# The high and low part of a weight side by side, and new start addresses for the moving operands

## The chip, the cores and the metric

The kernel runs on one core of one Trainium2 chip. The metric is the device time of one execution, in microseconds (us); three runs of the kernel before took 1782.89 to 1786.75 us, with a median of 1783.85 us.

## What is computed

The input is 512 tokens of 1024 channels, in float32. They pass a first block of two layers (a gated short convolution or latent attention with 8 heads, and each time a feed-forward part of width 2816 with a convolution over tokens) and a second block (three mixers side by side, then the same kind of feed-forward part). Nearly all of the work is in products of a weight matrix with the 512 tokens:

```python
def short_conv_mixer(x_n, w_in, conv_w, w_out):
    b, c, h = jnp.split(x_n @ w_in, 3, axis=-1)
    return (b * causal_dwconv(c * h, conv_w)) @ w_out

def conv_ffn(x_n, w_up, conv_w, w_down):
    g, u = jnp.split(causal_dwconv(x_n @ w_up, conv_w), 2, axis=-1)
    return (jax.nn.silu(g) * u) @ w_down
```

The largest are the three feed-forward parts, each with `w_up` of 1024 x 5632 and `w_down` of 2816 x 1024; then `a_w_in` (1024 x 3072), `a_w_out`, the projections of the attention (`w_dq`, `w_dkv`, `w_uq`, `w_ukv`, `w_o`) and of the second block (`w_in`, `w_out`).

## The kernel before

Channels lie on the 128 partitions and the 512 tokens along the free dimension, so an activation of 1024 channels is 8 tiles of 128 x 512. TensorE multiplies float32r operands, a rounded form of float32. To keep the precision, every operand is split into a high part (rounded to float32r) and a low part (the rest, also float32r), and a product is made of three matmuls in `mm3` (lines 157 to 159): high weight by high activation, low weight by high activation, high weight by low activation. In most products the weight is the stationary operand (128 x 128) and the activation the moving one (128 x 512); in `gemm_tok`, in `gating_in` and for the values in `layer_b` the roles are exchanged and the weight is moving.

Weights come through `slab`. A DMA on SyncE's queue brings up to 2048 columns into one of two `raw` buffers; the slab is then taken in pieces. For each piece ScalarE (ACT) casts `raw` into `whi` (line 147), and VectorE (DVE) subtracts `whi` from `raw` and writes `wlo` (line 149). `whi` and `wlo` are two tiles of the pool `wsp`, which has two buffers of each, and every word follows the one before it at a distance of 4 bytes. A piece of `w_up` has 1024 columns and feeds 24 matmuls, one of `w_down` has 1408 and feeds 33. Some pieces go to pools of their own instead (the argument `pool`): those are weights that must stay longer, such as the last pieces of a feed-forward part.

Activations that move through TensorE lie in the pool `xs` (the input of an up-projection, tiles `xsh` and `xsl`) and in `hid` (the input of a down-projection, `hidh` and `hidl`). The helper `pad` allocates a few bytes in front of a pool so that the next one begins at an address of choice; in the kernel before every moving operand and every weight tile begins at a multiple of 256 bytes. ACT and DVE also do the rest of the feed-forward part: the scaling, the convolution (line 282), the gate, the splits (lines 126 and 131), and in the first two feed-forward parts a matrix-vector product with `w_ada` on DVE (line 469).

The order of the instructions of each engine is made by a scheduler from priorities and a simulated timeline, not written by hand.

Of the kernel before, what the change touches and what calls it, by code (L numbers as in the profile page):

```python
# [12 lines left out]
F32R = mybir.dt.float32r  # L13
# [5 lines left out]
P = 128  # L19
# [10 lines left out]
PIECE = 1408  # L30
# [17 lines left out]
class Builder:  # L48
# [83 lines left out]
        else:  # L132
            self.done = nc.vector.scalar_tensor_tensor(vl, src, scale, vf, ALU.mult, ALU.subtract).ins

    def slab(self, src, piece, pool=None, width=PIECE):
        nc = self.nc
        n = src.shape[-1]
        raw = self.wraw.tile([P, SLAB], F32, tag="raw", name="raw")
        nc.sync.dma_start(raw[:, :n], src)
        for o in range(0, n, piece):  # L140
            own = pool[o // piece] if type(pool) is tuple else pool or self.wsp
            hi = own.tile([P, width], F32R, tag="whi", name="whi")
            lo = own.tile([P, width], F32R, tag="wlo", name="wlo")
            m = min(piece, n - o)
            s = slice(o, o + m)
            with self.tc.issue_after(self.rounded) if self.hold else nullcontext():
                nc.scalar.copy(hi[:, :m], raw[:, s])  # L147
            with self.tc.issue_after(self.hold) if self.hold else nullcontext():
                nc.vector.tensor_tensor(lo[:, :m], raw[:, s], hi[:, :m].bitcast(F32), ALU.subtract)  # L149
            if pool is None:  # L150
                yield hi, lo
            else:
                yield hi, lo, m
# [378 lines left out]
    def layer_b(self):  # L532
        nc = self.nc
        with ExitStack() as ctx:
# [27 lines left out]
            with ExitStack() as c2:  # L562
                v_pool = self.pool("v", 8, c2)
                k_pool, q_pool, r_pool = self.pool("k", 8, c2), self.pool("q", 8, c2), self.pool("r", 4, c2)
                self.ph = self.pool("ph_b2", 2, c2)
                o_pool = self.pool("o", 8, c2)

                def project(pr):
                    ks, vs, qs = [], [], []
                    for i, (wh, wl) in enumerate(self.slab(self.dr["w_uq"][pr], 512)):  # L570
                        ps = self.ps()
                        for k in range(4):
                            o = k * P
                            self.mm3(ps, wh[:, o:o + P], wl[:, o:o + P], *cq[k], k == 0, k == 3)
                        if i == 0:
                            x = self.t("sq", 2, self.tmp)
                            nc.scalar.copy(x, ps)
                        else:
                            qs.append(self.split(ps, q_pool, "q"))
                    (wh, wl), = self.slab(self.dr["w_ukv"][pr], 1024)  # L580
                    for i in range(2):
                        ps = self.ps()
                        for k in range(2):
                            o = (2 * i + k) * P
                            self.mm3(ps, wh[:, o:o + P], wl[:, o:o + P], *ckv[k], k == 0, k == 1)
                        ks.append(self.split(ps, k_pool, "k"))
                    for b in range(4):
                        ps = self.ps()[:, :256]
                        for k in range(2):
                            o = 512 + 256 * k  # L590
                            ch, cl = (t[:, b * P:(b + 1) * P] for t in ckv[k])
                            self.mm3(ps, ch, cl, wh[:, o:o + 256], wl[:, o:o + 256], k == 0, k == 1)
                        v = v_pool.tile([P, T], F32R, tag="v", name="v")
                        self.split_to(ps, v[:, :256], v[:, 256:])
                        vs.append(v)
                    qr = self.split(self.rope(x, cos, sin, self.done), r_pool, "r")
                    return ks, vs, qs, qr

                ready, outs = project(0), None
                for pr in range(5):  # L600
                    start = self.tc.tile_snap_priority()
                    mine = ready
                    if pr < 3:
                        ready = project(pr + 1)
                    if outs:
                        self.gemm(self.dr["w_o"], outs, self.add_h, (pr - 1,), 4)
                    if pr == 4:
                        break
                    ks, vs, qs, qr = mine
                    outs = []  # L610
                    with self.before(start):
                        for i in range(2):
                            r = slice(64 * i, 64 * i + 64)
                            outs.append(self.attend(qs[i], (qr[0][r], qr[1][r]), ks[i], (krh[r], krl[r]),
                                                    [(v[:, i * P:(i + 1) * P], v[:, 256 + i * P:256 + (i + 1) * P])
                                                     for v in vs], mask, o_pool))
# [54 lines left out]
    def gemm_tok(self, w, xs, n, kp, tok):  # L671

        ps = [self.ps() for _ in range(4)]
        k = 0
        for s in range(w.shape[0]):
            for hi, lo in self.slab(w[s], kp * n):
                for j in range(kp):
                    o = slice(j * n, j * n + n)
                    for b in range(4):
                        self.mm3(ps[b][:, :n], tok(xs[k][0], b), tok(xs[k][1], b), hi[:, o], lo[:, o],  # L680
                                 k == 0, k == KC - 1)
                    k += 1
        return ps
# [432 lines left out]
    def last_phase(self, y_b, wq, held, first, wf0, ctx):  # L1116

        with ctx:
            self.stat = self.pool("stat2", 1, ctx, space=PSUM)
            self.psum = self.pool("psum_f2", 7, ctx, space=PSUM)  # L1120
            self.xs = self.pool("xs2", 16, ctx)
            wf = self.pool("w_f", 1, ctx)
            add = self.summed(self.add_gated(16))
            n = 3 * P
            w = self.dr["w_out_b"]
# [46 lines left out]
    def ffn_phase(self, i, ctx):  # L1172
        self.stat = self.pool(f"stat{i}", 1, ctx, space=PSUM)
        with ExitStack() as ctx:
            self.xs = self.pool(f"xs{i}", 16, ctx)
            self.psum = self.pool(f"psum_f{i}", 7, ctx, space=PSUM)
            self.hid = self.pool(f"hid{i}", 28 - i, ctx)
            self.pad(480, ctx, side="right")
            self.ph = self.pool(f"ph_f{i}", 1, ctx, side="right")
# [129 lines left out]
```

## Time and profile before

| | |
|---|---|
| median of three runs | 1783.85 us |
| the execution that was profiled | 1781.47 us |
| its span from first to last instruction | 1779.5 us |
| TensorE matmul (PE) busy | 1749.2 us, 98% of the span |
| weight loads (PEld) busy | 1443.9 us, 81% |
| VectorE (DVE) busy | 1110.6 us, 62% |
| ScalarE (ACT) busy | 698.3 us, 39% |
| mean granted TensorE clock | 0.994 of full speed |

The profiled execution took 1.97 us more than its span. Matmuls overlap, and the length that the profile gives to one is modelled; what a matmul really costs in a stream is the distance from its start to the start of the next one. That distance is read from the timeline, where starts are printed to 10 ns, over several rows. TensorE's clock has two levels here, 1.2 and 2.4 GHz; a moving operand of 512 columns takes at least 512 cycles.

### The profile page before, as it was taken

To read this page: it belongs to the slowest core of one execution; us is meant where nothing else is said; L and a number is where in the kernel's file an instruction comes from. 1 tells how busy PE (TensorE), PEld (TensorE's weight loads), DVE (VectorE), ACT (ScalarE), POOL (GpSimd) and SP (SyncE) were. 2 spreads that over 40 slices of the span, in tenths; PEclk is the share of its full clock that TensorE was granted. 3 is DMA by queue.
4 is the path that set the end of the run, shared out by engine and by line. 5 is a ranking of instruction groups with operands and counts; after the bars stand their busy time and mean duration, and the time that the engine had idled before them with its cause. 6 is when DMAs were issued, how large, how long until landed. Compare 5 with 4: busy or idle time off the path is not lost.

```text
span 1779.5 us, 20603 instructions
## 1 busy us (share of the span) xinstructions
PE 1749.2 (98%) x8261; PEld 1443.9 (81%) x8261; DVE 1110.6 (62%) x1718; ACT 698.3 (39%) x1055; POOL 19.3 (1%) x27
## 2 busy tenths in 40 slices
PE   8999999999999999999999999999999999999998
PEld 7888888888887777787888888877867988888888
DVE  5655699447754676789953775764544766535554
ACT  4323335224433454443432443433354444314432
POOL 0000000000000000000000000100000000000000
PEclk9999999999999999999999999999989999999999
DMA  6222463322231211237423224312101222222231
GB/s 227 95 95 97 164 248 123 114 95 95 97 124 58 89 48 66 94 138 244 144 98 110 96 80 134 114 64 90 63 30 52 80 78 102 84 97 94 105 102 65
DMA packets 38927, 186.57 MB, mean 105 GB/s; under 512 B 5168, under 2 KB 6192, under 8 KB 26672
## 3 DMA queue, kind: packets, MB, share of 16 engines
q1 hardware_dynamic: 36720, 182.38, 29.6%
q10 hardware_dynamic: 2112, 2.89, 0.6%
q8 instruction: 64, 1.05, 0.2%
q14 instruction: 31, 0.25, 0.0%
HBM read 180.27 MB, written 2.10 MB: 102 GB/s over the span
## 4 chain that ended last, share of the span: by engine, by line
PE 90%; DVE 5%; DMA 3%; ACT 1%; issue 1%; POOLq 0%; DVEq 0%; SPq 0%; ACTq 0%
PE ps L157 27%; PE ps L158 27%; PE ps L159 27%; DMA ada<-w_ada 3%; DVE ada L469 2%; DVE wlo L149 1%; PE z L996 1%; PE z L164 1%; PE sc L157 1%; PE o L1004 1%; DVE cv L282 1%; PE sc L159 1%; PE sc L158 1%; PE pt L639 1%; PE sc L860 1%
## 5 line engine op out<-in xcount | busy, mean ns | idle before, releaser
L157 PE MATMUL ps<-xsh,whi 128*128 128x512 f32 (+1 forms) x1448 | 553.8, 387 | 9.7 <-ACT whi L147 6.0
L158 PE MATMUL ps<-xsh,wlo 128*128 128x512 f32 (+1 forms) x1448 | 560.4, 387 | 2.6 <-DVE wlo L149 2.6
L159 PE MATMUL ps<-xsl,whi 128*128 128x512 f32 (+1 forms) x1448 | 557.6, 386 | 0.0
L147 ACT CAST whi<-raw 128x1024 fp32r<-128x1024 f32 (+5 forms) x282 | 297.3, 1059 | 479.1 <-PE ps L159 390.6
L149 DVE TENSOR_TENSOR wlo<-raw,whi 128x1024 fp32r<-128x1024 f32 (+5 forms) x282 | 346.8, 1232 | 92.0 <-ACT whi L147 90.9
L157 PEld LDWEIGHTS ps<-xsh,whi 128*128 128x128 f32 x1448 | 273.4, 189 | 65.0 <-ACT whi L147 6.0
L158 PEld LDWEIGHTS ps<-xsh,wlo 128*128 128x128 f32 x1448 | 273.7, 189 | 60.0 <-DVE wlo L149 5.0
L159 PEld LDWEIGHTS ps<-xsl,whi 128*128 128x128 f32 x1448 | 272.9, 189 | 53.9 <-issue 0.3
L158 PE MATMUL ps<-hidh,wlo 128*128 128x512 f32 (+1 forms) x658 | 241.7, 368 | 0.0
L159 PE MATMUL ps<-hidl,whi 128*128 128x512 f32 (+1 forms) x658 | 241.6, 368 | 0.0
L157 PE MATMUL ps<-hidh,whi 128*128 128x512 f32 (+1 forms) x658 | 241.5, 368 | 0.0
L282 DVE SCALAR_TENSOR_TENSOR cv<-e,par,cv 128x511 f32<-128x511 f32 (+1 forms) x192 | 141.3, 745 | 2.0 <-ACT cv L278 0.3
L157 PEld LDWEIGHTS ps<-hidh,whi 128*128 128x128 f32 x658 | 124.0, 189 | 20.8
L158 PEld LDWEIGHTS ps<-hidh,wlo 128*128 128x128 f32 x658 | 124.0, 189 | 20.7
L159 PEld LDWEIGHTS ps<-hidl,whi 128*128 128x128 f32 x658 | 124.0, 189 | 20.3
L287 DVE TENSOR_TENSOR h<-ps,h 128x512 f32<-128x512 f32 (+1 forms) x75 | 49.9, 668 | 127.8 <-PE ps L159 127.5
L282 DVE SCALAR_TENSOR_TENSOR cv<-ps,par,cv 128x511 f32<-128x511 f32 (+1 forms) x88 | 65.5, 749 | 80.5 <-ACT cv L280 78.9
L414 DVE TENSOR_TENSOR e<-ps,rb 128x512 f32<-128x512 f32 x88 | 60.0, 687 | 57.2 <-PE ps L159 57.2
L126 ACT CAST hidh<-cv 128x512 fp32r<-128x512 f32 x66 | 40.8, 618 | 129.9 <-DVE cv L422 129.9
L278 ACT ACTIVATE cv<-e,par 128x512 f32<-128x512 f32 x96 | 69.0, 721 | 29.9 <-DVE e L414 28.5
L420 ACT ACTIVATE si<-cv 128x512 f32<-128x512 f32 x66 | 41.6, 631 | 75.1 <-DVE cv L282 75.1
L291 DVE SCALAR_TENSOR_TENSOR h<-ps,mod,h 128x512 f32<-128x512 f32 (+1 forms) x38 | 24.0, 636 | 67.5 <-PE ps L159 67.5
(311 smaller groups left out, 1752.7 us busy)
## 6 DMA issues: line engine op xcount, KB each, us to landing
raw<-w_up SPq DMA_DIRECT2D x65, 1024.0 KB, 4.7
raw<-w_down SPq DMA_DIRECT2D x48, 704.0 KB, 4.0
ada<-w_ada SPq DMA_DIRECT2D x48, 512.0 KB, 4.3
raw<-a_w_in SPq DMA_DIRECT2D x9, 1024.0 KB, 4.7
raw<-a_w_out SPq DMA_DIRECT2D x4, 1024.0 KB, 4.6
raw<-w_o SPq DMA_DIRECT2D x4, 1024.0 KB, 5.2
raw<-a_w_in_first SPq DMA_DIRECT2D x8, 384.0 KB, 3.8
raw<-w_uq SPq DMA_DIRECT2D x4, 768.0 KB, 4.8
```

Source lines behind the costliest of these rows:

```text
L126: nc.scalar.copy(vh, src)
L147: nc.scalar.copy(hi[:, :m], raw[:, s])
L149: nc.vector.tensor_tensor(lo[:, :m], raw[:, s], hi[:, :m].bitcast(F32), ALU.subtract)
L157: mm(ps, wh, xh, start=first, stop=False)
L158: mm(ps, wl, xh, start=False, stop=False)
L159: mm(ps, wh, xl, start=False, stop=last)
L278: nc.scalar.activation(y, x, AF.Identity, scale=self.p(w, 2 * n + i))
L282: nc.vector.scalar_tensor_tensor(y[:, k:], x[:, :T - k], self.p(w, (2 - k) * n + i), y[:, k:], ALU.mult, ALU.add)
L287: self.nc.vector.tensor_tensor(self.h[m][:, s], ps, self.h[m][:, s], ALU.add)
L414: nc.vector.tensor_tensor(e, ps, rb, ALU.mult)
L420: nc.scalar.activation(st["s"], y, AF.Silu)
L469: nc.vector.scalar_tensor_tensor(w, w, 1.0, ca, ALU.mult, ALU.mult, accum_out=self.mod[:, i:i + 1])
```

## The change

`slab` gets an argument `apart`. Without it (and without a pool of its own) the two parts of a piece are now one tile of 128 x 1408 x 2 words: word 2j is the high part of column j and word 2j + 1 the low part. So ACT writes the high part with a step of 8 bytes, DVE reads it and writes the low part with that step, and TensorE loads either part as a stationary operand with a step of 8 bytes. Where the weight is the moving operand (`w_ukv`, and `gemm_tok`), `apart=True` keeps the two parts as two contiguous halves of one tile. Weights with a pool of their own stay as they were. The space is the same.

Four more pads shift the moving operands. Modulo 256 bytes, `xs` and `hid` begin at 0 and 128 in the first layer and feed-forward part, at 64 and 192 in the second feed-forward part, and at 192 and 0 in the third; the attention, and the mixers of the second block, stay at 0.

```diff
-    def slab(self, src, piece, pool=None, width=PIECE):
+    def slab(self, src, piece, pool=None, width=PIECE, apart=False):
         nc = self.nc
         n = src.shape[-1]
         raw = self.wraw.tile([P, SLAB], F32, tag="raw", name="raw")
         nc.sync.dma_start(raw[:, :n], src)
         for o in range(0, n, piece):
-            own = pool[o // piece] if type(pool) is tuple else pool or self.wsp
-            hi = own.tile([P, width], F32R, tag="whi", name="whi")
-            lo = own.tile([P, width], F32R, tag="wlo", name="wlo")
+            if pool is None and apart:
+                t = self.wsp.tile([P, 2, width], F32R, tag="w", name="w")
+                hi, lo = t[:, 0], t[:, 1]
+            elif pool is None:
+
+                t = self.wsp.tile([P, width, 2], F32R, tag="w", name="w")
+                hi, lo = t[:, :, 0], t[:, :, 1]
+            else:
+                own = pool[o // piece] if type(pool) is tuple else pool
+                hi = own.tile([P, width], F32R, tag="whi", name="whi")
+                lo = own.tile([P, width], F32R, tag="wlo", name="wlo")
...
-                    (wh, wl), = self.slab(self.dr["w_ukv"][pr], 1024)
+                    (wh, wl), = self.slab(self.dr["w_ukv"][pr], 1024, apart=True)
...
-            for hi, lo in self.slab(w[s], kp * n):
+            for hi, lo in self.slab(w[s], kp * n, apart=True):
...
             self.psum = self.pool("psum_f2", 7, ctx, space=PSUM)
+            self.pad(192, ctx)
             self.xs = self.pool("xs2", 16, ctx)
+            self.pad(64, ctx)
             wf = self.pool("w_f", 1, ctx)
...
         with ExitStack() as ctx:
+            if i:
+                self.pad(64, ctx)
             self.xs = self.pool(f"xs{i}", 16, ctx)
             self.psum = self.pool(f"psum_f{i}", 7, ctx, space=PSUM)
+            self.pad(128, ctx)
             self.hid = self.pool(f"hid{i}", 28 - i, ctx)
```

Of the order of instructions, the start of the program on TensorE shows what is typical of a piece. The names are output, moving and stationary operand; a wait in brackets names the engine that is waited for. Before:

```order
L157 MATMUL ps<-xsh,whi 128x512 [waits Activation_49]
L157 MATMUL ps<-xsh,whi 128x512 x5
L158 MATMUL ps<-xsh,wlo 128x512 [waits DVE_49]
L159 MATMUL ps<-xsl,whi 128x512
L158 MATMUL ps<-xsh,wlo 128x512
```

After the change, at the same place (lines are 8 further down, and both parts are called `w`):

```order
L165 MATMUL ps<-xsh,w 128x512 [waits Activation_49]
L165 MATMUL ps<-xsh,w 128x512 x5
L166 MATMUL ps<-xsh,w 128x512 [waits DVE_49]
L167 MATMUL ps<-xsl,w 128x512
L166 MATMUL ps<-xsh,w 128x512
```

Order and waits are the same: although the two parts are one tile now, the first matmul still waits for ACT's high part alone, and the low part is waited for where it is read.

In the attention of the first block the scheduler arrives at another order. On TensorE, where the scores (`sc`) of the first head pair are interleaved with the projection of the next pair's queries (`ps<-lath`), there stood before:

```order
L157 MATMUL sc<-krh,rh 128x128
L157 MATMUL sc<-krh,rh 128x256
L158 MATMUL sc<-krh,rl 128x128
L159 MATMUL sc<-krl,rh 128x128
L158 MATMUL sc<-krh,rl 128x256
L159 MATMUL sc<-krl,rh 128x256
L157 MATMUL ps<-lath,whi 128x512
```

and now:

```order
L165 MATMUL sc<-krh,rh 128x128
L165 MATMUL sc<-krh,rh 128x256
L166 MATMUL ps<-lath,w 128x512
L167 MATMUL ps<-latl,w 128x512
L165 MATMUL ps<-lath,w 128x512
```

The four remaining score matmuls of the first two blocks moved eleven rows back, behind matmuls of the projection. Such exchanges are found all through the attention; outside it the engines' orders are the same but for the names.

## Rows read from the trace of the kernel before

**Rows 1.** The page's busy times, and its row of the granted clock by slices.

```profile
span 1779.5 us, 20603 instructions
PE 1749.2 (98%) x8261; PEld 1443.9 (81%) x8261; DVE 1110.6 (62%) x1718; ACT 698.3 (39%) x1055; POOL 19.3 (1%) x27
...
PEclk9999999999999999999999999999989999999999
```

**Rows 2.** Who TensorE waited for: us in total, times, longest.

```profile
PE ps L157 <- ACT whi L147: 6.9, 2, 6.0
...
PE ps L158 <- DVE wlo L149: 2.6, 3, 1.6
```

**Rows 3.** Timeline of matmuls in a down-projection: start, us, what; 17 left out stand alike.

```profile
901.49 0.39 PE L157 MATMUL ps<-hidh,whi 128*128 128x512 f32 x1
901.72 0.39 PE L158 MATMUL ps<-hidh,wlo 128*128 128x512 f32 x1
...
905.80 0.39 PE L158 MATMUL ps<-hidh,wlo 128*128 128x512 f32 x1
```

**Rows 4.** Timeline of the weight loads there: one of them.

```profile
901.72 0.19 PEld L159 LDWEIGHTS ps<-hidl,whi 128*128 128x128 f32 x1
```

**Rows 5.** Timeline of the first matmuls, at the start of the program; four between these.

```profile
9.18 0.63 PE L159 MATMUL ps<-xsl,whi 128*128 128x512 f32 x1
...
11.31 0.63 PE L158 MATMUL ps<-xsh,wlo 128*128 128x512 f32 x1
```

**Rows 6.** Timeline around the end of the second feed-forward part.

```profile
1123.24 0.28 PE L157 MATMUL ps<-hidh,whi 128*128 128x256 f32 x1
...
1123.60 0.28 PE L330 MATMUL st<-ones,last 128*128 128x1 f32 x2
...
1123.97 0.36 PE L330 MATMUL st<-ones,last 128*128 128x1 f32 x2
...
1125.08 0.36 PE L157 MATMUL ps<-hidh,whi 128*128 128x256 f32 x1
```

**Rows 7.** Timeline of matmuls with 128 columns in the attention.

```profile
653.10 0.22 PE L157 MATMUL o<-pth,v 128*128 128x128 f32 x1
653.16 0.28 PE L158 MATMUL o<-pth,v 128*128 128x128 f32 x1
653.27 0.27 PE L159 MATMUL o<-ptl,v 128*128 128x128 f32 x1
```

**Rows 8.** The load of weights for the second of them.

```profile
653.10 0.19 PEld L158 LDWEIGHTS o<-pth,v 128*128 128x128 f32 x1
```

**Rows 9.** Two matmuls of plain float32 operands (timeline), and their group (busy, mean ns).

```profile
1319.43 1.02 PE L1004 MATMUL o<-w,vn 128*128 128x512 f32 x2
...
L1004 PE MATMUL o<-w,vn 128*128 128x512 f32 x12 | 6.2, 596 | 0.0
```

**Rows 10.** Stages: window, length, busy PE, PEld, DVE, ACT (and count), POOL, clock.

```profile
185.00:318.00 133.00, 132.79 (x592) 109.57 (x592) 116.61 (x168) 54.83 (x71) 1.01 (x1) 1.00 0.52 179
595.00:615.00 20.00, 17.41 (x89) 13.91 (x89) 14.93 (x24) 9.25 (x18) 0.00 (x0) 1.00 0.31 93
765.00:901.00 136.00, 133.64 (x594) 109.71 (x593) 122.56 (x184) 57.00 (x76) 1.01 (x1) 1.00 0.51 174
1403.00:1537.00 134.00, 133.99 (x679) 115.25 (x679) 85.70 (x122) 60.48 (x84) 0.87 (x1) 0.99 0.21 74
```

**Rows 11.** Split of weights: groups of the largest form (busy, mean ns, idle before).

```profile
L147 ACT CAST whi<-raw 128x1024 fp32r<-128x1024 f32 x201 | 210.6, 1050 | 282.3 <-PE ps L159 227.4 <-issue 30.3 <-DMA raw<-w_down 8.7
L149 DVE TENSOR_TENSOR wlo<-raw,whi 128x1024 fp32r<-128x1024 f32 x201 | 245.0, 1220 | 47.5 <-ACT whi L147 47.1
```

**Rows 12.** Writes of `yh`, `yl`, two of three with 16-byte step: min/median/max ns.

```profile
L126 ACT CAST yh<-st x3: 586/1091/1093, 1285.3 to 1300.1; 128x512 fp32r<-128x512 f32 x3
L131 DVE TENSOR_TENSOR yl<-st,yh x3: 690/1048/1087, 1286.4 to 1300.7; 128x512 fp32r<-128x512 f32 x3
```

**Rows 13.** DVE's subtraction for weights alone, in one stage (busy, count).

```profile
765.00:901.00 136.00, 29.63 (x24) 1.00 0.51 174
```

## The prediction

> **What bounds the kernel now.** The page comes first: TensorE's matmuls are busy for 1749.2 of 1779.5 us, at full clock in all slices but one, and no other engine is busy for more than 62% [rows 1]. The list of waits says how much TensorE lost to others: the longest entry for ACT's cast of weights is 6.9 us, of which 6.0 us are the start of the program, and for DVE's low part 2.6 us [rows 2]. So the time is the number of matmuls times the distance between their starts, and I read that distance next. In the timeline of a down-projection the starts at 901.49 and 905.80 us are 19 matmuls apart [rows 3]: 4.31/19 = 226.8 ns; I use 226.7. At 2.4 GHz, 512 columns need 213.3 ns. So 13.3 ns of each matmul, 6%, are something other than columns.
>
> The next views say when this excess is there. At the start of the program the clock is still at 1.2 GHz: from 9.18 to 11.31 us are 5 matmuls, 426 ns each, and 512/1.2 is 426.7 [rows 5]: no excess. Matmuls of plain float32 take twice as long per column. The group's mean length is 596 ns and two of them cover 1.02 us [rows 9], so the second starts 0.42 to 0.43 us after the first: no excess worth the name either. With 256 columns, three matmuls take from 1123.24 to 1123.60 us, 120 ns each [rows 6], which is 106.7 + 13.3: the excess belongs to the matmul, not to its columns. And with 128 columns one matmul takes 653.10 to 653.16 us [rows 7]: 60 ns against 53.3, about half the excess.
>
> What goes on beside each of these is the load of the next matmul's weights: the load for the matmul after starts with the matmul itself [rows 4, 8]. How long a load takes is seen where a matmul has one moving column and the load alone sets the pace: 1123.97 to 1125.08 us holds five pairs of such matmuls, 111 ns each [rows 6]. So the matmul of 60 ns had half a load beside it and half the excess; those of 120 and 226.7 ns had a whole load and the whole excess. I conclude that reading weights holds up the reading of the moving operand, and only where the moving operand is read at its full rate of 2048 bytes in 213 ns, 9.6 bytes/ns in each partition. Weights that lie side by side are read at 512 bytes in 111 ns, 4.6 bytes/ns. The two slow cases are those in which both walk through memory at about one speed (2048 bytes in 427 ns are 4.8 bytes/ns).
>
> **The change part by part.** *Step of 8 bytes in the weight load.* A load now walks over 1024 bytes in 111 ns, 9.2 bytes/ns: the speed of the moving operand. If they hold each other up when they come to the same part of memory, the slower one is now no longer overtaken again and again during a load; once one has given way, they keep their distance. No row shows a weight load with a step. Bounds: 13.3 ns less (213.3, the excess gone, as in [rows 5, 9]) and 13.3 ns more (240.0: a load with this step touches twice as much memory, so if each piece of memory touched costs the moving operand something, the excess doubles). I take 8.9 ns less, two thirds of the excess: the rows at equal speeds show none, but they are at half the rate, where a hold-up could hide, so I don't take all of it.
>
> How many matmuls read weights with the step: of 512 columns 144 + 432 (`a_w_in`), 1056 + 1056 + 960 (three `w_up`; 96 of the third have pools of their own), 120 (`w_dq`, `w_dkv`), 336 (`w_vp`, `w_cqk`, `w_bqk`), 192 (`a_w_out`), 495 + 429 + 429 (`w_down`), 144 (`w_uq`), 192 (`w_o`), 120 (`w_out_ac`), 27 (`w_out_b`): 6132; of 256 columns 132 + 54 = 186. The excess is the same for both. 6318 x 8.9 ns = 56.2 us less; the bounds are 84 us less and 84 us more.
>
> *TensorE's other loads* (scores, values, weights with their own pools) keep their step: nothing.
>
> *Start addresses.* All operands began at 0 modulo 256, so no row shows another start. The shifts change which part of memory moving operand and weights come to together; the bounds are those above, and I take nothing besides.
>
> The Trainium skill, TensorE: Matmul & The Clock Gate, "Wait — 56ns, not 53.3ns?", gives the start-to-start distance of 512 columns as 512/1.2 GHz when cold and 215.7 ns when warm, 2.5 ns over the columns. The cold figure agrees with this trace's 426 ns, the warm one does not: 226.7 here. If the change brought the distance to the page's figure, the sum would be 6318 x 11 = 69 us instead of 56.
>
> *ACT and DVE with a step of 8 bytes.* ACT now writes with it, DVE reads and writes with it. The nearest rows have a step of 16 bytes: for 512 elements ACT takes 1092 ns instead of 586, DVE up to 1087 instead of 690 [rows 12]. So 1024 elements cost between nothing and 1.0 us more on ACT (now 1.05), and between nothing and 0.8 us more on DVE (now 1.22) [rows 11]. A piece of 1024 columns is split while TensorE works on the piece before, 24 x 226.7 ns = 5.4 us; cast and subtraction take 2.3 us of this now and 4.1 us at the upper bound. This cover holds where DVE is free. It is tight in the up-projections of the first two feed-forward parts, where DVE also multiplies `w_ada`: 116.6 of 133 us and 122.6 of 136 us busy, against 85.7 of 134 in the third [rows 10], 24 subtractions in each stage [rows 13]. At the upper bound 24 x 0.8 = 19 us come on top there, DVE needs 136 and 142 us, and those two stages are its own. With TensorE at 217.8 ns they would last 128 and 131 us, so the upper bound costs 8 + 11 = 19 us. 8 bytes is nearer to 4 than to 16, so I take a quarter, 5 us. What is queued behind a longer subtraction on DVE is the scaling of the next output (line 414) that frees a bank of PSUM for TensorE.
>
> *Waits.* The first matmul of a piece waits for ACT, and the first with a low part for DVE, as before, so the common tile adds none. *The attention's new order:* TensorE idles 2.6 us where its first scores begin (the window of 20 us) [rows 10]; the score matmuls that moved back give it projections to do there or delay them. Bound by that idle time on both sides; I take nothing.
>
> *Sum.* 1781.5 (the profiled execution) - 56.2 + 5 = 1730.3 us. That execution is 2.4 us under the median of the runs, so in terms of the median: **1733 us**, 2.8% faster.
>
> **The rivals.**
>
> *The weight load pays by the memory it touches.* A load with the step touches 1024 bytes instead of 512. If the moving operand pays for the memory that a load touches, the excess doubles to 26.7 ns, the distance is 240.0 ns and the time 1784 + 84 = 1868 us. For it: the excess follows the load, half a load half the excess [rows 7], which a price per piece gives as well as an overtaking does. Against it: at half the rate of the moving operand nothing is seen of such a price [rows 5, 9], though it could be hidden. It decides as soon as, at equal speed, the share of the touched memory that collides does not fall below half of today's. The Trainium skill, SBUF — State Buffer, "Specifications (TRN2)", speaks for it: SBUF's lines have 16 bytes, and each cross to a new line pays a penalty. The same section of the Trainium skill asks for two hits in a line for full bandwidth, which a step of 8 bytes just keeps; by that the price on ACT and DVE would be nothing and the sum 5 us lower; no row here shows either.
>
> *Equal speed holds them together in the wrong place.* If moving operand and weights begin in the same part of memory and stay there, each read of a load collides. Then some of the four starts are slow and others fast, and it is the place, not the step, that matters. With two of the six large products slow (some 1500 matmuls, 13.3 ns more) and the rest unchanged: + 20 us, 1804. Against it: whichever gives way is then behind, and out of step.
>
> *Nothing changes on TensorE.* The excess could be a price for each word of weights, of which there are 128 with or without the step. The same rows allow it. Then the time is 1784 us plus what DVE loses, 0 to 5 us.
>
> *DVE becomes the bound* in the two stages named above, at 8 + 11 us: with the gain on TensorE, 1747 us; it only weakens the forecast.
>
> **How the numbers follow.** The excess shrinks: 0.58, with its own range from 1702 us (all of it gone, little lost on DVE) to 1765 (a third of it gone, DVE at its upper bound). A price for each word: 0.15, of which 0.09 within 0.2%, 0.03 to either side. Pay by memory touched: 0.18, slower. The wrong place: 0.09, of which 0.06 slower and 0.03 near nothing. Together: faster 0.61, within 0.2% (3.6 us, about what a measurement of this kernel can tell from no change) 0.12, slower 0.27. The range reaches from 1702 over the unchanged time to 1798; what it leaves out is nearly all of the slow case.
>
> **What would show it.** Right: starts in a down-projection 216 to 220 ns apart, the same for every start address, unchanged in the matmuls of the scores and of the weights with pools of their own; ACT's cast of 1024 under 1.3 us and DVE's subtraction under 1.5 us; no more than 5 us of new waits of TensorE for `w`. Wrong: 226.7 as before (a price for each word), 240 (for memory touched), or distances that differ from one feed-forward part to the next by the start of its moving operand. On the side of DVE: a subtraction near 2 us and TensorE idle behind it in the two stages with `w_ada`.

## The result, and the profile after

The changed kernel takes 1814.89 us (median of four runs), the kernel before 1783.37 (four runs): a ratio of 1.0174 with an interval from 1.0154 to 1.0194, slower by 31.5 us. Forecast were 1733 us and a range from 1702 to 1798.

The page's busy times and its row of the granted clock answer to [rows 1]:

```profile
span 1812.5 us, 20594 instructions
PE 1782.3 (98%) x8261; PEld 1482.3 (82%) x8261; DVE 1112.2 (61%) x1718; ACT 716.2 (40%) x1055; POOL 18.4 (1%) x27
...
PEclk9999999999999999999999999999989999999999
```

PE is still busy for 98% of the span, at the same clock (0.994 of full speed in both), but for 33 us longer, and the span grew by 33.0 us. Was it waiting? The list of waits of TensorE (us in total, times, longest) answers to [rows 2]:

```profile
PE ps L165 <- ACT w L155: 6.1, 1, 6.1
...
PE ps L166 <- DVE w L157: 1.1, 3, 0.6
```

No: 6.1 and 1.1 us, against 6.9 and 2.6 before. So it is the distance between starts. The timeline of matmuls (start, us, what) in four places answers to [rows 3]; each pair is 18 matmuls apart:

```profile
249.98 0.39 PE L167 MATMUL ps<-xsl,w 128*128 128x512 f32 x1
...
254.18 0.39 PE L167 MATMUL ps<-xsl,w 128*128 128x512 f32 x1
...
339.92 0.40 PE L166 MATMUL ps<-hidh,w 128*128 128x512 f32 x1
...
344.09 0.39 PE L166 MATMUL ps<-hidh,w 128*128 128x512 f32 x1
...
922.02 0.39 PE L166 MATMUL ps<-hidh,w 128*128 128x512 f32 x1
...
926.16 0.39 PE L166 MATMUL ps<-hidh,w 128*128 128x512 f32 x1
...
1000.01 0.39 PE L165 MATMUL ps<-xsh,w 128*128 128x512 f32 x1
...
1004.20 0.40 PE L165 MATMUL ps<-xsh,w 128*128 128x512 f32 x1
```

The first pair is the first up-projection (moving operand at 0): 4.20/18 = 233.3 ns. Then the first down-projection (at 128): 4.17/18 = 231.7. Then the second down-projection (at 192): 4.14/18 = 230.0. Last the second up-projection (at 64): 4.19/18 = 232.8, which at starts printed to 10 ns is the same as the first. Before, all of these stood at 226.7.

The third up-projection (at 192) has two paces. The timeline of its first part and, behind a stretch of its down-projection, of its second part, each pair again 18 matmuls apart:

```profile
1559.42 0.39 PE L166 MATMUL ps<-xsh,w 128*128 128x512 f32 x1
...
1563.56 0.39 PE L166 MATMUL ps<-xsh,w 128*128 128x512 f32 x1
...
1639.84 0.40 PE L166 MATMUL ps<-xsh,w 128*128 128x512 f32 x1
...
1644.04 0.40 PE L166 MATMUL ps<-xsh,w 128*128 128x512 f32 x1
```

These are 4.14/18 = 230.0 ns and 4.20/18 = 233.3 ns with the same start, 192. The stretch of the down-projection between them (at 0) ran at 233.3, and the up-projection behind it stayed there.

Over all matmuls of 512 columns with weights from `wsp` (6086 distances between 200 and 245 ns), what lies above 226.7 ns adds up to 35.6 us in the kernel after and to 2.4 us in the kernel before. The difference, 33.2 us, covers the whole of the 33.0 us by which the span grew.

Matmuls of 256 columns with the step did not change; this answers to [rows 6] (9 matmuls in 1.09 us, 121 ns):

```profile
1145.68 0.28 PE L165 MATMUL ps<-hidh,w 128*128 128x256 f32 x1
...
1146.77 0.28 PE L165 MATMUL ps<-hidh,w 128*128 128x256 f32 x1
```

The groups of the weight loads, before and after, and of the split (busy us, mean ns, idle before) answer to [rows 4, 11]:

```profile
L158 PEld LDWEIGHTS ps<-xsh,wlo 128*128 128x128 f32 x1448 | 273.7, 189 | 60.0 <-DVE wlo L149 5.0 <-issue 1.0
...
L166 PEld LDWEIGHTS ps<-xsh,w 128*128 128x128 f32 x1368 | 266.6, 195 | 55.8 <-DVE w L157 2.8 <-issue 0.3
```

```profile
L155 ACT CAST w<-raw 128x1024 fp32r<-128x1024 f32 x189 | 212.3, 1124 | 294.9 <-PE ps L167 259.4 <-issue 34.4 <-ACT s L641 0.6
```

```profile
L157 DVE TENSOR_TENSOR w<-raw,w 128x1024 fp32r<-128x1024 f32 x189 | 230.9, 1222 | 52.3 <-ACT w L155 51.8 <-issue 0.3
```

A load is recorded with 195 ns instead of 189, ACT's cast takes 74 ns more, DVE's subtraction 2 ns more.

### The profile page after: what moved, and what is told of

It reads as the page before. It is cut to its first block, busy times and chain, and to the rows that moved or that the text cites. A ratio compares the mean times of both kernels' runs of the same rounds, so it can differ in the third digit from the quotient of the medians.

```text
span 1812.5 us, 20594 instructions
## 1 busy us (share of the span) xinstructions
PE 1782.3 (98%) x8261; PEld 1482.3 (82%) x8261; DVE 1112.2 (61%) x1718; ACT 716.2 (40%) x1055; POOL 18.4 (1%) x27
## 4 chain that ended last, share of the span: by engine, by line
PE 94%; DVE 3%; DMA 2%; ACT 1%; issue 1%; POOLq 0%; DVEq 0%; SPq 0%; ACTq 0%
PE ps L165 28%; PE ps L166 28%; PE ps L167 28%; DMA ada<-w_ada 1%; PE z L172 1%; PE z L1004 1%; PE sc L165 1%; PE o L1012 1%; DVE ada L477 1%; PE sc L166 1%; PE sc L167 1%; PE pt L647 1%; PE sc L868 0%; DVE w L157 0%; PE st L963 0%
## 5 line engine op out<-in xcount | busy, mean ns | idle before, releaser
L165 PE MATMUL ps<-xsh,w 128*128 128x512 f32 x1368 | 536.7, 397 | 10.8 <-ACT w L155 6.1
L166 PE MATMUL ps<-xsh,w 128*128 128x512 f32 x1368 | 542.0, 396 | 1.1 <-DVE w L157 1.1
L167 PE MATMUL ps<-xsl,w 128*128 128x512 f32 x1368 | 540.6, 396 | 0.0
L155 ACT CAST w<-raw 128x1024 fp32r<-128x1024 f32 (+4 forms) x262 | 299.5, 1143 | 472.8 <-PE ps L167 427.6
L157 DVE TENSOR_TENSOR w<-raw,w 128x1024 fp32r<-128x1024 f32 (+4 forms) x262 | 326.1, 1245 | 94.3 <-ACT w L155 93.5
L165 PEld LDWEIGHTS ps<-xsh,w 128*128 128x128 f32 x1368 | 266.5, 195 | 65.0 <-ACT w L155 6.1
L166 PEld LDWEIGHTS ps<-xsh,w 128*128 128x128 f32 x1368 | 266.6, 195 | 55.8 <-DVE w L157 2.8
L167 PEld LDWEIGHTS ps<-xsl,w 128*128 128x128 f32 x1368 | 266.4, 195 | 52.9 <-issue 0.3
L166 PE MATMUL ps<-hidh,w 128*128 128x512 f32 (+1 forms) x559 | 214.9, 385 | 0.0
L165 PE MATMUL ps<-hidh,w 128*128 128x512 f32 (+1 forms) x559 | 214.8, 385 | 0.0
L167 PE MATMUL ps<-hidl,w 128*128 128x512 f32 (+1 forms) x559 | 214.7, 385 | 0.0
L166 PEld LDWEIGHTS ps<-hidh,w 128*128 128x128 f32 x559 | 108.8, 195 | 19.4 <-DVE w L157 0.4
L165 PEld LDWEIGHTS ps<-hidh,w 128*128 128x128 f32 x559 | 108.8, 195 | 19.1
L167 PEld LDWEIGHTS ps<-hidl,w 128*128 128x128 f32 x559 | 108.7, 195 | 19.0
```

What stands on the lines that cost most here:

```text
L165: mm(ps, wh, xh, start=first, stop=False)
L166: mm(ps, wl, xh, start=False, stop=False)
L167: mm(ps, wh, xl, start=False, stop=last)
```

## The experiments

Two theories stood at the start. A: the step in the weight load makes each matmul of 512 columns slower, whatever the starts. B: the new starts do it, and the step helps or does nothing. Each is a part of the change, so each was run alone.

**The step alone** (`e1_step_only`): the kernel after without the four pads.

```diff
-            self.pad(192, ctx)
             self.xs = self.pool("xs2", 16, ctx)
-            self.pad(64, ctx)
...
-            if i:
-                self.pad(64, ctx)
...
-            self.pad(128, ctx)
```

> The step of 8 bytes in the weights alone; all moving operands begin at 0 modulo 256 as before. Theory A (the weight load makes the moving operand pay for the memory that it touches, start addresses matter little): the distance of 512 columns is 233.3 ns in every stage, as it already is after the change where the start is 0, so 6132 x 6.6 = 40 us over before, 1824 us. Theory B (the start addresses are what costs, the step helps or is neutral): no slower than before, 1784 us or less.

Measured: 1818.34 us, ratio 1.0203 (1.0181 to 1.0225), 36 us slower. Nearly all distances are 233.3 ns; above 226.7 they add up to 40.0 us (35.6 in the whole change).

**The starts alone** (`e2_starts_only`): the kernel before with the same four pads.

> The four pads alone, weights contiguous as before. Theory A: 1784 us, or a little less: with contiguous weights the few matmuls of 256 columns that begin at 192 took 117.5 instead of 120 ns after the change; 2.5 ns on some 3130 matmuls would be 8 us, 1776 us. Theory B: 1815 us as after the change.

Measured: 1794.15 us, ratio 1.0068 (1.0050 to 1.0085), 12 us slower. Neither theory had this: with contiguous weights the starts cost by themselves, with the step they win back some 4 us (31.5 against 36 us; above 226.7 ns, 35.6 against 40.0). Here the distances above 226.7 add up to 18 us, 16 more than before, and the span grew by 13; the other 3 us come back elsewhere, in small pieces that were not followed up. The timeline of this kernel in the third up-projection (moving operand at 192), 18 matmuls apart:

```profile
1639.89 0.39 PE L157 MATMUL ps<-xsh,whi 128*128 128x512 f32 x1
...
1644.09 0.39 PE L157 MATMUL ps<-xsh,whi 128*128 128x512 f32 x1
```

That is 4.20/18 = 233.3 ns without any step, as slow as with it.

**Bare streams** (`m1_stream`): streams of 96 matmuls, one for each pair of step and start.

> This kernel leaves the whole computation out: streams of 96 matmuls in the order of the three products, one stream for each step of the weights, start of the moving operand and number of columns, with nothing else running. Theory A: 226.7 ns with contiguous weights at every start, 233 with a step of 8 bytes at every start, more with 12 and 16 bytes. Theory B: with either step the distance depends on the start, below 220 ns at some of them and above 230 at others. For both, the load alone (8 columns) shows whether a step makes the load itself longer than 111 ns.

The names of the groups tell the step in words (s), the starts of moving operand (m) and weights (w) in bytes, and the columns (n); columns are busy us, mean ns and idle before:

```profile
L59 PE MATMUL s1x_m64x_w64x_n512x<-m,w 128*128 128x512 f32 x96 | 22.1, 391 | 0.1
...
L59 PE MATMUL s1x_m192x_w0x_n512x<-m,w 128*128 128x512 f32 x96 | 22.7, 397 | 0.1
...
L59 PE MATMUL s1x_m0x_w64x_n512x<-m,w 128*128 128x512 f32 x96 | 22.7, 396 | 0.1
...
L59 PE MATMUL s2x_m0x_w0x_n512x<-m,w 128*128 128x512 f32 x96 | 22.7, 395 | 0.1
...
L59 PE MATMUL s4x_m128x_w0x_n512x<-m,w 128*128 128x512 f32 x96 | 23.4, 404 | 0.1
```

A stream's busy time holds 95 distances, so 0.6 us between two streams are 6.3 ns in each. Weights and moving operand both at 64: fast. One at 192 and the other at 0, or one at 0 and the other at 64: slow, and as slow as the step. So the start of the moving operand counts relative to that of the weights. Since nothing else runs in these streams, ACT's and DVE's work is not needed for the slow pace. Mean distances from start to start (ns, 512 columns):

| moving start minus weight start | 0 | 32 | 64 | 96 | 128 | 160 | 192 | 224 |
|---|---|---|---|---|---|---|---|---|
| contiguous weights | 226.7 | 233.3 | 228.9 | 233.3 | 232.4 | 234.3 | 233.4 | 233.3 |
| step of 8 bytes | 233.3 | 233.4 | 233.3 | 233.3 | 231.4 | 233.3 | 230.0 | 232.1 |

With contiguous weights the kernel before stood at the best of these starts (one of 240 bytes gives 226.7 too). With the step no start comes below 230.0. At 384 and 256 columns and start 0 the step costs nothing (173.3 and 120.0 ns with and without it); at 256 columns and start 192 it does, 120.0 against 113.4. Theory A is right in sign but wrong in "whatever the starts", and B is wrong about the step.

**Does it need two operands that walk?** (`m2_walk`)

> Leaves the computation out: streams of 96 matmuls as before, now also with a step of 0 (one word read again and again) for the weights, the moving operand or both, with other numbers of columns, other starts, and with matmuls of 8 columns between those of 512, under which the load of the next weights is laid bare. Theory A (what collides are places in memory): where one of the two does not walk, the excess falls from 13.3 to under 5 ns. Theory C (the weight load takes a share of TensorE's reading whatever it reads; a price for each word or for the time of the load): 226.7 ns also with a step of 0 for the weights. The load laid bare: about 107 to 111 ns with a step of 4 or 8 bytes if a load is as fast with either, some 7 ns longer with 8 bytes if the longer load itself is what was paid for.

An operand walks when it is read at one address after the other. Moving operand of one word read over and over (v0), weights of one word (s0), and pairs of a matmul of 512 and one of 8 columns:

```profile
L63 PE MATMUL s0x_v1x_m0x_w0x_n512x<-m,w 128*128 128x512 f32 x96 | 22.5, 395 | 0.1
...
L63 PE MATMUL s1x_v0x_m0x_w0x_n512x<-m,w 128*128 128x512 f32 x96 | 21.1, 380 | 0.1
...
L63 PE MATMUL pair_s3x<-m,w 128*128 128x512 f32 x48 | 19.8, 544 | 0.1
...
L63 PE MATMUL pair_s2x<-m,w 128*128 128x512 f32 x48 | 17.0, 486 | 0.1
...
L63 PE MATMUL pair_s1x<-m,w 128*128 128x512 f32 x48 | 16.5, 476 | 0.1
```

A moving operand of one word gives 216.7 ns, with either step. Weights of one word leave 231.6 ns. So most of the excess needs a moving operand that walks, but it does not need the weights to walk. That speaks against theory A's fight over the same place in memory, and against theory C, which wanted 226.7. A pair, which holds a matmul of 512 columns and two loads, is 10 ns longer with the 8-byte step ((17.0 - 16.5)/48) and 69 ns longer with 12 bytes ((19.8 - 16.5)/48). Of the 10 ns some 6.6 would be the matmul's own, if it pays here as in the streams of 512 columns alone. The load by itself is seen better in the streams of 128 columns, where the columns do not set the pace (192 columns give the same 111.7 ns): 111.7 ns with contiguous weights, 117.8 (start 0) and 120.0 (start 192) with the 8-byte step. So the load is 6 to 8 ns longer, about what a matmul of 512 pays; that the one is the reason for the other is not shown, and at 256 and 384 columns and start 0 the same load costs nothing.

The Trainium skill, TensorE: Matmul & The Clock Gate, "Wait — 56ns, not 53.3ns?", has 215.7 ns for 512 columns when warm. The trace comes near it, with 216.7, only where the moving operand stays on one word or, as the windows below show, within 32 bytes. The Trainium skill, SBUF — State Buffer, "Specifications (TRN2)", asks for two hits in each 16-byte line. The load agrees in the main: with 8 bytes, where two words still lie in a line, it grows by 6 to 8 ns, and it gets much longer with 12 bytes, where fewer than two do on average.

**All at 192** (`e3_step_all_192`): the step, with the moving operands of all feed-forward parts at the start that was best with it. Against the kernel after:

```diff
             self.pad(192, ctx)
             self.xs = self.pool("xs2", 16, ctx)
...
-            self.pad(480, ctx, side="right")
+            self.pad(480 + 64, ctx, side="right")
             self.hid = self.pool("hid2", 28, ctx, side="right")
...
-            if i:
-                self.pad(64, ctx)
+            self.pad(192, ctx)
             self.xs = self.pool(f"xs{i}", 16, ctx)
...
-            self.pad(128, ctx)
```

> The step of 8 bytes, and all operands from xs and hid in the feed-forward parts and the first layer at 192 modulo 256, the start at which the bare stream with this step took 230.0 instead of 233.3 ns. If the distances of the bare streams carry over to the kernel: 5193 matmuls x 3.3 + 939 x 6.7 = 23 us over before, 1806 us, 12 us under the step alone. If the start is a matter of what else goes on in a stage: like the step alone, 1818 us.

Measured: 1805.35 us, ratio 1.0125 (1.0107 to 1.0143), 23 us slower. The total fits, the inside does not, so the fit is partly luck: the first layer and the feed-forward parts run at 230.0 ns up to 204 us, at 233.3 up to 513 us, then at 230.0 again but for the end of the second down-projection, with the same starts. The timeline shows that last place, where the pace turns:

```profile
1098.99 0.39 PE L166 MATMUL ps<-hidh,w 128*128 128x512 f32 x1
...
1103.13 0.40 PE L165 MATMUL ps<-hidh,w 128*128 128x512 f32 x1
1103.36 0.42 PE L166 MATMUL ps<-hidh,w 128*128 128x512 f32 x1
1103.63 0.40 PE L167 MATMUL ps<-hidl,w 128*128 128x512 f32 x1
...
1107.13 0.40 PE L167 MATMUL ps<-hidl,w 128*128 128x512 f32 x1
```

Up to 1103.13 are 18 matmuls in 4.14 us, 230.0 ns. From 1103.36 the next start is 263 ns away in the trace (0.27 as printed): one matmul, the first of a new piece that reads the low part, takes some 30 ns more. From then on 15 matmuls take 3.50 us, 233.3 ns. The timeline of the loads says what came late, here and at the other turn, at 513 us (in brackets the load's idle time and whom it waited for):

```profile
512.36 0.19 PEld L166 LDWEIGHTS ps<-hidh,w 128*128 128x128 f32 x1 [0.15 <-DVE w L157]
...
1103.28 0.19 PEld L166 LDWEIGHTS ps<-hidh,w 128*128 128x128 f32 x1 [0.18 <-DVE w L157]
```

The loads around them start together with the matmul before their own, as in [rows 4]; these two start 0.13 and 0.15 us behind it (the matmuls began at 512.23 and 1103.13), because DVE's low part was not ready. At 513 us the matmuls lost under 10 ns by it and turned from 233.3 to 230.0, at 1103 us some 30 ns and turned from 230.0 to 233.3. (The turn at 204 us stands behind eight short matmuls.) A late load need not turn the pace: in the changed kernel one that was 0.16 us late in the second down-projection, at 1109.8 us, left it at 230.0. So the addresses do not set the pace alone, and what shifts a load in time can turn it.

**Only the weights moved, and everything moved** (`e5_weights_at_64`, `e6_all_at_64`): the kernel before, all weights contiguous. The first moves `wsp`, and with it `wraw`, `tmp` and `small`, by 64 bytes and puts what follows back; the second leaves out the second line, so that most moving operands move along.

```diff
-        self.pad(288)
+        self.pad(352)
         self.wraw = self.pool("wraw", 2)
...
-        self.pad(64)
+        self.pad(256)
```

> The kernel before with one pad 64 bytes longer ahead of the weights and the next one lengthened to put everything behind back where it was: weights stay contiguous and no moving operand of the large products moves, but 6180 matmuls of 512 columns and 186 of 256 now have their moving operand 192 bytes behind the weights, modulo 256. Theory: only the relative start counts, 233.4 instead of 226.7 ns: + 41.2 us, less 1.2 us for 256 columns: about 1823 us, ratio 1.022, as slow as the 8-byte step alone without any step. Rival (the starts of the moving operands themselves are what counted in the run of the starts alone): 1783, no change.

> The kernel before with one pad 64 bytes longer ahead of the weights, so that weights and moving operands of the first layer, of both first feed-forward parts and of the third's up-projection all begin at 64 modulo 256. Theory (relative start): those stay at 226.7 ns; only what lies on the other side of the memory (the third down-projection, latents: 888 matmuls of 512 columns, 252 of 256) gets 6.7 ns more or less: + 4 us, about 1787. Rival (a moving operand that begins at 64 costs 2.2 ns, wherever the weights are): + 14 us, 1797.

Measured: 1818.57 us, ratio 1.0205 (1.0191 to 1.0219), for the weights alone, and 1784.33 us, ratio 1.0013 (1.0004 to 1.0022), for all. Two numbers in the sources, with no step and the same order of matmuls, cost as much as the step alone. Both times are near those of the theory that only the relative start counts (1823 and 1787 us) and away from its rivals' (1783 and 1797). Timeline of the first, 18 matmuls apart in the first up-projection (4.20/18 = 233.3 ns), and its loads:

```profile
250.02 0.39 PE L159 MATMUL ps<-xsl,whi 128*128 128x512 f32 x1
...
254.22 0.39 PE L159 MATMUL ps<-xsl,whi 128*128 128x512 f32 x1
```

```profile
L158 PEld LDWEIGHTS ps<-xsh,wlo 128*128 128x128 f32 x1448 | 273.8, 189 | 64.0 <-issue 1.0 <-DVE wlo L149 0.2
```

The loads have 189 ns here as in the kernel before, so the slow pace does not need a longer load. In the second, the same place (4.07/18 = 226.1 ns; starts are printed to 10 ns, so 226.7 as before):

```profile
249.94 0.39 PE L157 MATMUL ps<-xsh,whi 128*128 128x512 f32 x1
...
254.01 0.39 PE L157 MATMUL ps<-xsh,whi 128*128 128x512 f32 x1
```

The stretches of the programs side by side, from the first matmul of one to the first of the next (us; `x` are the 480 matmuls of the second part of `w_up`, `h` the 264 of the first part of `w_down`; 3.2/480 = 6.7 ns):

| | before | after | step alone | starts alone | all at 192 | weights moved | all moved |
|---|---|---|---|---|---|---|---|
| first h | 59.9 | 61.1 | 61.6 | 61.6 | 61.6 | 61.6 | 59.8 |
| first x | 108.8 | 112.0 | 112.0 | 108.8 | 112.0 | 112.0 | 108.8 |
| second h | 59.8 | 60.7 | 61.6 | 61.6 | 60.8 | 61.6 | 59.8 |
| second x | 108.8 | 112.0 | 112.0 | 109.8 | 110.4 | 112.0 | 108.8 |
| third h | 59.9 | 61.6 | 61.6 | 59.9 | 60.7 | 61.6 | 61.6 |
| third x | 108.8 | 112.0 | 112.0 | 112.0 | 110.4 | 112.0 | 108.9 |

In the last column one stretch is slow: the third down-projection, whose moving operand did not move along with the weights.

**How far must the moving operand walk?** (`m3_windows`)

> The kernel's own computation is left out: streams of 96 matmuls of 512 columns. The moving operand reads a window of few words over and over (2 to 256 words; one word alone gave 216.7 ns), with weights contiguous, with the 8-byte step, or one word. Theory of collisions by place: the excess needs both to come to the same part of memory in turns, so a window of 16 words (64 bytes) that stays in one place has a smaller excess with all weights than 226.7, and one that depends on the window's start, and with one word of weights the distance depends on whether the window is in the word's place: near 216.7 where it isn't. Rival (walking itself costs, wherever the weights are): 226 to 232 with every window, at every start.

The names tell the words of weights (W1: one word), the words of the window (M), the step (s) and the window's start (m):

```profile
L64 PE MATMUL W1x_M16x_s1x_m0x<-m,w 128*128 128x512 f32 x96 | 23.6, 408 | 0.1
...
L64 PE MATMUL W128x_M32x_s1x_m0x<-m,w 128*128 128x512 f32 x96 | 23.0, 401 | 0.1
...
L64 PE MATMUL W128x_M64x_s2x_m0x<-m,w 128*128 128x512 f32 x96 | 22.7, 395 | 0.1
...
L64 PE MATMUL W128x_M64x_s1x_m0x<-m,w 128*128 128x512 f32 x96 | 22.1, 390 | 0.1
...
L64 PE MATMUL W128x_M8x_s1x_m0x<-m,w 128*128 128x512 f32 x96 | 21.1, 380 | 0.1
```

Neither theory holds. Windows of 8, 16 and 32 bytes give 216.7 ns, as one word does. A window of 64 bytes is slower than a full walk: 243.3 ns with weights of one word at each of the four starts tried, 238 to 242 with 128 contiguous words. 128 bytes give 236.6, and from 256 bytes on all is as in a full walk: 226.7, and 233.3 with the step. A window of 64 bytes next to a single word of weights is among the slowest, and as slow at each of four starts, so a collision by place does not explain it (with 128 words the start still matters a little); since windows up to 32 bytes cost no more than one word, walking as such does not cost either.

**One short matmul in the middle** (`m4_disturbed`)

> The kernel's own computation is left out: 48 streams of 96 matmuls of 512 columns, in whose middle one matmul has fewer columns (8 to 504) and so shifts the moment at which the following ones meet their weight loads. In the run with every start at 192 the same pair of addresses ran at 230.0 ns for some 100 us and at 233.3 for some 300, and went from one to the other at one matmul that came 30 ns late. Theory (the pace is set by when a load falls against the moving operand's reading, and is kept until something shifts it): with the 8-byte step at 192 the second halves of the streams run at 230.0 or at 233.3, depending on the columns of the one matmul; with contiguous weights at start 0 they all return to 226.7, since the kernel before keeps 226.7 throughout, whatever interrupts it. Rival (the pace of a stream is set by addresses alone, and what changed it in that run was something else, such as DMA traffic): each pair of step and start has one pace, before and behind the short matmul.

Timeline of the stream with the 8-byte step at 192 and one matmul of 8 columns in its middle; the view joins matmuls of one name into a row (start, us to the end of the last, count), one row ahead of the short one and one behind it:

```profile
945.37 10.05 PE L53 MATMUL s2x_m192x_c8x<-m,w 128*128 128x512 f32 x43
...
956.53 9.96 PE L53 MATMUL s2x_m192x_c8x<-m,w 128*128 128x512 f32 x42
```

Without the last matmul's 0.39 and 0.40 us these are 9.66/42 = 230.0 ns and 9.56/41 = 233.2 ns. One short matmul turned the pace for the rest of the stream. The six others (96 to 504 columns) left it at 230.0. A second pair turns more often: contiguous weights and a moving operand at 128. Its stream with one matmul of 96 columns, a row ahead and a row behind:

```profile
425.22 10.16 PE L53 MATMUL s1x_m128x_c96x<-m,w 128*128 128x512 f32 x43
...
438.12 8.10 PE L53 MATMUL s1x_m128x_c96x<-m,w 128*128 128x512 f32 x34
```

These are 9.77/42 = 232.6 ns and 7.70/33 = 233.3 ns; matmuls of 200, 448 and 504 columns turned it in the same way, those of 8, 296 and 384 did not. With contiguous weights at start 0, the pace came back to 226.7 after each of the seven, in most of them behind a few distances of up to 236 ns; at 192 contiguous it stayed at 233.3, and with the step at 0 and 128 it did not turn either. So the theory held for the pair that it was made for in one of seven cases, and for another pair in four of seven. The rival, one pace for each pair, falls with both.

**A version of the kernel before with better starts** (`e4_pieces_apart`): pads of 64 bytes ahead of the weight pools that are read with 256 columns alone, since the streams gave 113.3 instead of 120.0 ns there; the pad of 192 puts what follows back.

```diff
+            self.pad(64, first)
             wf = self.pool("w_f0", 3, first)
...
+            self.pad(192, ctx)
             self.xs = self.pool("xs2", 16, ctx)
+            self.pad(64, ctx)
             wf = self.pool("w_f", 1, ctx)
...
+                self.pad(64, ctx)
                 late = self.pool("late1", 4, ctx)
```

> The kernel before (contiguous weights, moving operands of the large products at 0), with pads of 64 bytes ahead of the weight pools of the second and third feed-forward part that are read with 256 columns alone, so that there the moving operand begins 192 bytes behind the weights, modulo 256. In the bare streams this gave 113.3 instead of 120 ns per matmul of 256 columns. If that carries over, 456 matmuls gain 6.7 ns each: 3.0 us less, about 1780 us for the same runs of before, ratio 0.998; the stretch around the end of the second feed-forward part shrinks by 1.8 us and that at the end of the third as much. If relative starts only matter at 512 columns: no change, 1783.

Measured: 1779.69 us against 1782.09, ratio 0.9989 (0.9980 to 0.9998). The sign fits, but 2.4 us is less than 0.2%, and in the trace these matmuls have 117 to 118 ns, not 113.3: 456 of them gain about 1 us. The bare stream's figure did not carry over here, and this is not a version to recommend. It can: in the run with everything moved, 196 matmuls of 256 columns at the end of the third down-projection, 192 bytes behind their weights as well, took 113.8 ns on average.

## Why the prediction was wrong, point by point

*What bounds the kernel* was right: TensorE's pace is the time, and the change of that pace (33.2 us) covers the 33.0 us by which the span grew.

*The step of 8 bytes* is the step that failed: "the slower one is now no longer overtaken again and again during a load", 8.9 ns less on 6318 matmuls. Measured are 6.6 ns more where the starts are equal, 36 us instead of -56, and nothing on the matmuls of 256 columns at start 0, where "the excess is the same for both" was assumed. The picture behind it, two readers that hold each other up when they come to the same part of memory, does not hold: the excess stays with weights of one word and is largest with a moving operand of 64 bytes. The reading of [rows 6 to 9], that the excess goes with the load of weights beside the matmul, was a correlation. Its 60 ns for 128 columns, "about half the excess", was one distance; the next in [rows 7] is 110, and a stream of such matmuls runs at 111.7. What the experiments show in its place: with the step a matmul of 512 columns takes 230.0 to 233.4 ns at each of the eight starts of the table, where 226.7 stood before. What they support as the reason, without showing it: the pace depends on how the reading of the moving operand and the load fall against each other in time. The start relative to the weights, the step, the columns and a single late load or short matmul can each shift it. The kernel before sat at the best of these relations, to which the bare stream came back after each of seven interruptions. The change left it.

*Start addresses* ("I take nothing besides") failed too: with contiguous weights they cost 12 us alone. "All operands began at 0 modulo 256, so no row shows another start" was a reason for a wider range, not for zero. In the change the two do not add: 36 and 12 us apart, 31.5 together, because the starts 128 and 192 can be better than 0 once the step is there: they were in two down-projections and in half of the third up-projection.

*ACT and DVE* were over-priced: 5 us were taken, ACT paid 74 ns for a cast of 1024 and DVE 2 ns, and TensorE's waits for `w` did not grow. The 16-byte rows [rows 12] were the wrong neighbour.

*Waits and the attention's order*: right. The waits of the list changed by under 2 us.

*The sum of the range.* Its end of 1765 us for "a third of it gone, DVE at its upper bound" is some 5 us low by its own terms: 1784 - 28 + 14 (less is gained on TensorE, so DVE's upper bound costs 14) are 1770.

*The rivals.* "Pays by the memory it touches" had the sign, not the size (1868 us) nor the mechanism: steps of 12 and 16 bytes touch more still and give 235 to 240 ns in the streams, not a multiple. "Equal speed holds them together in the wrong place" came nearest in time (1804 us) and named "the place, not the step", but it too was a collision by place, and the step alone cost more than the starts alone. "Nothing changes on TensorE" and "DVE becomes the bound" fall.

*Still open*: what unit makes a moving operand wait when it goes beyond 32 bytes, why 64 bytes are the worst window, and why the step costs at 512 columns and not, at start 0, at 256 or 384. That the timing decides is inferred from the pairs of addresses with two paces, from the late loads at two turns and from the windows; the unit that waits was not seen in any run. No run set the moment of a load and nothing else.

## What to carry to other kernels

Before a layout is changed, look at whether the engine's pace is already at the best figure that any address gives: a stream of a hundred matmuls for each pair of starts and steps says it in one run, and here it would have shown that 226.7 ns was the best of all that were tried. Take such a figure as a lead and not as a price: some pairs have two paces, and the 256-column figure did not carry over into one kernel. Shift weights and moving operands together or not at all; a pad in front of one pool can cost 2% without any change of instructions. Where a term is put at zero because no row shows it, its range must be as wide as the effect that it is part of.

## What was unexpected

- The distance of 512-column float32r matmuls depends on the start of the moving operand relative to the weights, modulo 256 bytes: 226.7 to 234.3 ns in steps of 16 bytes, up to 238.9 at starts that are no multiple of 16 (4 and 244 bytes gave 238.4 and 238.9).
- One pair of addresses can have two paces, 230.0 and 233.3 ns, each kept for hundreds of matmuls. Two of the turns stand right behind a weight load that started 0.13 to 0.15 us late.
- A moving operand that stays within 32 bytes runs at 216.7 ns, one that repeats 64 bytes at 238 to 243 ns with contiguous weights or one word of them.
- A moving operand with a step of 8 bytes runs at 451 ns in the streams, so that `apart` is needed where the weight moves.
